# Values made token-major by VectorE's 32x32 block transposition and DMAs by way of DRAM, in a decoder layer on one core

## The chip, the core and the metric

The kernel runs on one core of a Trainium2 chip. A core has five engines with instruction streams of their own: TensorE (PE in the profile: matrix products from SBUF into PSUM; PEld is its weight load), VectorE (DVE), ScalarE (ACT), GpSimd (POOL) and SyncE (SP, which here only issues DMAs). Each engine works its instructions off in order and waits on semaphores for the others. PSUM has eight banks of 128 partitions x 512 numbers. The metric is the device time of one execution in microseconds (us). The kernel before takes 1237.49 us (median of 3 runs, 1237.15 to 1237.61).

## The reference, cut to what matters

One decoder layer on 272 tokens (16 learned ones and 256 of the input), width 2048, all in float32. Two groups of heads share one input projection: four mLSTM heads (values 256 wide) and eight retention heads (values 128 wide).

```python
u = rmsnorm(h, norm_mix)
proj = u @ w_in
q_r, k_r, v_r, g_r, q_m, k_m, v_m, o_m, i_pre, f_pre = split(proj)
# retention: rotary(q), rotary(k); P = (q k^T) * decay;  o = P v
ret = head_norm(o, ret_norm) * silu(g_r)
# mLSTM: causal conv of 4 and silu on q, k; P = (q k^T) * exp(D - m)
hm = head_norm((P v) / max(|sum P|, exp(-m)), mlstm_norm) * sigmoid(o_m)
h = h + concat(ret, hm) @ w_out
u = rmsnorm(h, norm_ffn)
gate, val = split(causal_dwconv(u @ w_up, 3 taps))
h = h + (silu(gate) * val) @ w_down
return rmsnorm(h, norm_final)[:, 16:]
```

`head_norm` takes a head's mean over its value columns away and divides by the root of the variance. The kernel computes attention over all 272 tokens at once, without the chunks and the recurrent state.

## The kernel before, in words

**Layout.** Activations lie with features on the 128 partitions and tokens along the free dimension ("feature-major"). A product `project` makes 128 features of 256 to 272 tokens: the 2048 x 128 weight tile comes as two halves of 512 KB. Each half (`load_w`) is loaded into `wraw`, ScalarE rounds it to `whi` (L129), VectorE takes the remainder `wlo` (L131), and TensorE does 24 products of 128x128 weights: 16 with `whi` on the two parts of the activations (L138, L139), 8 with `wlo` (L141). There are 4 buffers of `wraw`, 5 of `whi` and 5 of `wlo`, so loads and rounding can run some halves ahead of TensorE.

**Stages.** First the input is loaded and split, while the products for the gates and for the first mLSTM head's k and q are made (L208 to L235). Then come the projections of the four mLSTM heads and of the eight retention heads. A head's attention (`ml_attend`, `ret_attend`) is written one head later, so that its small steps can run beside the next head's projections. Then the output projection (L536), the up projection with its convolution (L628) and the down projection (L673).

**The factor rstd.** The input's normalisation is applied after the products: `rstd1` (128 copies of the 272 factors) multiplies what is read from PSUM. It comes from the sum of squares: ScalarE squares `hT` (L246), VectorE adds (L249, L254), a product with `inv_dm` (L256) sums over the partitions, and ScalarE and VectorE make the inverse root (L164 to L169, L258). Until `rstd1` is there, no finished projection can leave PSUM. The pool `mm` has four banks: one holds the first head's q, the next three hold its two value tiles and its first gate; the fifth projection, the second gate, needs the bank of q back, which L416 frees.

**Values.** The weighting product `weigh` needs the values with tokens on the partitions ("token-major"). `values` gets them by six products with the identity per mLSTM head and three per retention head (L324, 272 tokens are blocks of 128, 128 and 16) into banks of the pool `at`. VectorE sums each token's values out of PSUM (L327, L328), scales that to minus the mean (L329, L330), and ScalarE copies the values with the mean taken off into the one buffer `vpad` (L333).

**Order.** The program is written head by head, but each engine's order is fixed when it is built, by a list scheduler that plays the program through on durations of its own; `issue_after` and `high_priority` are hints for it. So a change in one place can move instructions of others. Buffers (`bufs`) are reused in turn, each by a wait for the last reader.

Of the kernel before, what the change touches and what calls it, by code (L numbers as in the profile page):

```python
# [16 lines left out]
P = 128  # L17
# [6 lines left out]
NQ = T - T0  # L24
# [59 lines left out]
def trunk(ctx: ExitStack, tc: tile.TileContext, io, out: bass.AP):  # L84
    nc = tc.nc

    def pool(name, bufs, **kw):
        return tc.tile_pool(name=name, bufs=bufs, **kw)
# [4 lines left out]
    at = ctx.enter_context(pool("at", 4, space=PSUM))  # L93

# [112 lines left out]
    with pool("sq", 1, side="right") as sqp:  # L207
        for k0, k1 in [(0, 1), (1, 2)] + [(k, k + 2) for k in range(2, KT, 2)]:  # L208
            n = k1 - k0
            nc.sync.dma_start(hT[:, k0:k1, :], io["xT"][:, k0:k1, :])  # L210
            if k0 == 0:
                nc.sync.dma_start(par[:, 0:KT], io["par"][:, 0:KT])
            raw = wpool.tile([P, 2, W0], F32, name="wraw", bufs=4)[:, :n, :]
            last_load = nc.sync.dma_start(raw, io["w0"][:, k0:k1, :])
            for k in range(k0, k1):
                nc.scalar.activation(xh[:, k, :], hT[:, k, :], AF.Copy, scale=pcol("gmix", k))
                nc.vector.scalar_tensor_tensor(out=xl[:, k, :], in0=hT[:, k, :], scalar=pcol("gmix", k),
                                               in1=xh[:, k, :].bitcast(F32), op0=ALU.mult, op1=ALU.subtract)

            hi = wpool.tile([P, 2, W0 + GW], F32R, name="whi", bufs=5)[:, :n, :]  # L220
            copied = nc.scalar.copy(hi[:, :, 0:W0], raw)
            lo = wpool.tile([P, 2, 2 * P], F32R, name="wlo", bufs=5)[:, :n, :]
            nc.vector.tensor_tensor(out=lo, in0=raw[:, :, 0 : 2 * P], in1=hi[:, :, 0 : 2 * P].bitcast(F32), op=ALU.subtract)
            parted = nc.vector.tensor_tensor(out=hi[:, :, W0:], in0=raw[:, :, 2 * P :], in1=hi[:, :, 2 * P : W0].bitcast(F32), op=ALU.subtract)
            for k in range(k0, k1):
                i = k - k0
                first, last = k == 0, k == KT - 1
                for j, (ps, t0) in enumerate(((k_ps, 0), (q_ps, TQ))):
                    w = hi[:, :, j * P : (j + 1) * P], lo[:, :, j * P : (j + 1) * P]
                    mmk(ps[:, : T - t0], w, [(i, k)], lambda k: xh[:, k, t0:], lambda k: xl[:, k, t0:], 0, KT - 1)  # L230
                if not last:
                    nc.tensor.matmul(gates_ps[:, :T], hi[:, i, 2 * P :], xh[:, k, :], start=first, stop=False)
                nc.tensor.matmul(gates_ps[0:GW, :T], hi[:, i, 2 * P : W0], xl[:, k, :], start=False, stop=False)
                if last:
                    nc.tensor.matmul(gates_ps[:, :T], hi[:, i, 2 * P :], xh[:, k, :], start=False, stop=True)  # L235
        with tc.issue_after(last_load.ins):
            nc.sync.dma_start(par[:, KT:NPAR0], io["par"][:, KT:NPAR0])

        v0_ps = project(next(tiles), xh, xl, 0)
# [12 lines left out]
        with tc.high_priority():  # L252
            for n in (2, 1):
                nc.vector.tensor_tensor(out=sum4[:, 0:n, :], in0=sum4[:, 0:n, :], in1=sum4[:, n : 2 * n, :], op=ALU.add)  # L254
            ms = at.tile([P, 512], F32, name="atps")
            nc.tensor.matmul(ms[:, :T], inv_dm, sum4[:, 0, :], start=True, stop=True)  # L256
            r = rsqrt_m2(wk, ms[:, :T], T, squared)
            nc.vector.tensor_scalar(out=rstd1, in0=r[:, :T], scalar1=-0.5, scalar2=None, op0=ALU.mult)  # L258
# [12 lines left out]
    rB, rA, rM, rm, rones = map(row, ("rB", "rA", "rM", "rm", "rones"))  # L271
# [41 lines left out]
    def values(vts):  # L313

        w = P * len(vts)
        blocks = ((0, P), (P, P), (2 * P, CC))
        pss = [at.tile([P, 512], F32, name="atps"), None]
        if 3 * w > 512:
            pss[1] = at.tile([P, 512], F32, name="atps")
        where = []  # L320
        for b, (s0, n) in enumerate(blocks):
            ps, c0 = (pss[1], 0) if (b == 2 and pss[1] is not None) else (pss[0], b * w)
            for j, vt in enumerate(vts):
                nc.tensor.transpose(ps[0:n, c0 + j * P : c0 + (j + 1) * P], vt[:, s0 : s0 + n], ident)  # L324
            where.append(ps[0:n, c0 : c0 + w])
        nm = wk.tile([P, 3], F32, name="nm")
        nc.vector.reduce_sum(nm[:, 0:2], pss[0][:, 0 : 2 * w].rearrange("p (a e) -> p a e", a=2), axis=mybir.AxisListType.X)  # L327
        nc.vector.reduce_sum(nm[0:CC, 2:3], where[2], axis=mybir.AxisListType.X)  # L328
# [3 lines left out]
        for b, (s0, n) in enumerate(blocks):  # L332
            nc.scalar.activation(v[0:n, b, :], where[b], AF.Identity, bias=nm[0:n, b : b + 1])  # L333
        return v
# [44 lines left out]
    def ret_project(h):  # L379
        decay = wk.tile([P, ABC], F32, name="e")  # L380
        nc.gpsimd.dma_start(decay, io["decay"][h])
# [12 lines left out]
    def ret_attend(h, kT, qT, vT, g, decay):  # L394
        v = values([vT])
# [43 lines left out]
    def ml_attend(h, kT, qT, vTs, gs):  # L439
        v = values(vTs)  # L440
# [32 lines left out]
        for j in range(2):  # L473
            o = weigh(lambda b: v[:, b, j * P : (j + 1) * P], pT)
            hj = wk.tile([P, NQ], F32, name=f"hj{j}", bufs=1)
# [315 lines left out]
```

## Time and profile before

One profiled execution, and three timed ones.

| What | Value |
|---|---|
| timed, median of 3 (range) | 1237.49 us (1237.15 to 1237.61) |
| the profiled execution, its time | 1237.72 us |
| its span, from first to last instruction | 1236.0 us |
| PE busy, share of the span | 1225.0 us, 99% |
| DVE, ACT, POOL busy | 832.6, 656.9, 66.8 us |
| mean granted TensorE clock | 0.998 |
| DMA, mean over the span | 181 GB/s |
| products with the identity for the values (L324) | 48, of 273 ns each, overlapping |

A row of the timeline has the start, the length (both us), the engine, the line, the operation, output<-input, shapes, and xN for N merged instructions; in square brackets the idle time before it and what ended it. Products overlap: each is some 0.28 us long, but the next one starts 0.12 us after it. A row of the windows has the window (us from the span's start), its length, and then busy time and instruction count of each engine, the granted clock, the DMA share and GB/s.

### The profile page before, as it was taken

What the parts mean: (1) busy time and instruction counts of PE and PEld (TensorE: products, weight loads), DVE (VectorE), ACT (ScalarE), POOL (GpSimd) and SP (SyncE); (2) the same over time, 40 slices, a digit from 0 to 9 for tenths busy, and PEclk for the clock granted to TensorE, in tenths of its full rate; (3) what the DMA queues carried; (4) which work ended last, traced back from release to release, by engine and by line L of the source; (5) the groups of instructions that cost most, each with busy time, mean ns of one, the idle gap of its engine ahead of it and who ended that gap; (6) DMA issues with size and microseconds to landing.
All of it is one profiled execution on the core that took longest, in us unless ns stands there. A gap on an engine that the chain in (4) does not pass through costs nothing.

```text
span 1236.0 us, 22256 instructions
## 1 busy us (share of the span) xinstructions
PE 1225.0 (99%) x9086; PEld 1174.6 (95%) x9086; DVE 832.6 (67%) x1227; ACT 656.9 (53%) x880; POOL 66.8 (5%) x71
## 2 busy tenths in 40 slices
PE   9999999999999999999999999999999999999997
PEld 9999999999999999999999998888999999998886
DVE  7957777766665766778878764445677677674452
ACT  8756756555556556555555543334555555554442
POOL 0200011111110110000000000000000000000000
PEclk9999999999999999999999999999999999999999
DMA  8755555555554656555556556566565555566661
GB/s 271 256 185 154 161 154 161 172 174 161 177 167 132 207 186 212 184 185 179 184 183 185 180 183 187 187 187 188 187 186 176 185 187 177 183 187 182 187 210 69
DMA packets 63687, 224.30 MB, mean 181 GB/s; under 512 B 7392, under 2 KB 8544, under 8 KB 63456
## 3 DMA queue, kind: packets, MB, share of 16 engines
q1 hardware_dynamic: 62640, 219.59, 57.0%
q0 software_dynamic: 656, 2.76, 0.8%
q8 instruction: 71, 1.16, 0.4%
q10 hardware_dynamic: 288, 0.52, 0.1%
q14 instruction: 32, 0.26, 0.1%
HBM read 220.75 MB, written 2.10 MB: 180 GB/s over the span
## 4 chain that ended last, share of the span: by engine, by line
PE 97%; DVE 1%; DMA 1%; ACT 1%; issue 0%; SPq 0%; DVEq 0%; ACTq 0%
PE mmps L138 24%; PE mmps L139 24%; PE mmps L141 24%; PE atps L658 7%; PE atps L659 7%; PE atps L662 7%; PE atps L347 1%; PE atps L339 0%; DMA wraw<-in_w 0%; PE atps L324 0%; DMA wraw<-in_wi 0%; PE atps L348 0%; DVE wlo L131 0%; PE atps L340 0%; ACT whi L129 0%
## 5 line engine op out<-in xcount | busy, mean ns | idle before, releaser
L129 ACT CAST whi<-wraw 128x1024 fp32r<-128x1024 f32 x404 | 423.2, 1049 | 475.5 <-PE mmps L139 255.4
L131 DVE TENSOR_TENSOR wlo<-wraw,whi 128x1024 fp32r<-128x1024 f32 x404 | 495.0, 1226 | 192.4 <-ACT whi L129 187.3
L139 PE MATMUL mmps<-ul,whi 128*128 128x258 f32 x1408 | 345.8, 283 | 0.0
L138 PE MATMUL mmps<-uh,whi 128*128 128x258 f32 x1408 | 345.5, 282 | 0.0
L138 PEld LDWEIGHTS mmps<-uh,whi 128*128 128x128 f32 x1408 | 266.1, 189 | 0.1
L139 PEld LDWEIGHTS mmps<-ul,whi 128*128 128x128 f32 x1408 | 265.1, 188 | 0.1
L138 PE MATMUL mmps<-xh,whi 128*128 128x272 f32 (+2 forms) x880 | 223.5, 287 | 0.4 <-DVE cx L416 0.4
L139 PE MATMUL mmps<-xl,whi 128*128 128x272 f32 (+2 forms) x880 | 223.2, 287 | 0.0
L141 PE MATMUL mmps<-uh,wlo 128*128 128x258 f32 x1408 | 198.9, 284 | 0.0
L141 PEld LDWEIGHTS mmps<-uh,wlo 128*128 128x128 f32 x1408 | 182.4, 189 | 0.0
L138 PEld LDWEIGHTS mmps<-xh,whi 128*128 128x128 f32 x880 | 165.6, 188 | 0.6 <-issue 0.6
L139 PEld LDWEIGHTS mmps<-xl,whi 128*128 128x128 f32 x880 | 166.0, 189 | 0.0
L658 PE MATMUL atps<-whi,mh 128*128 128x512 f32 (+1 forms) x360 | 140.5, 391 | 0.0
L659 PE MATMUL atps<-whi,ml 128*128 128x512 f32 (+1 forms) x360 | 140.2, 390 | 0.0
L141 PE MATMUL mmps<-xh,wlo 128*128 128x272 f32 (+2 forms) x880 | 129.1, 285 | 0.0
L141 PEld LDWEIGHTS mmps<-xh,wlo 128*128 128x128 f32 x880 | 116.4, 188 | 0.1
L662 PE MATMUL atps<-wlo,mh 128*128 128x512 f32 (+1 forms) x360 | 110.8, 388 | 0.0
L572 DVE TENSOR_TENSOR cu<-mmps,rstd 128x258 f32<-128x258 f32 x88 | 37.6, 427 | 97.5 <-PE mmps L141 97.0
L658 PEld LDWEIGHTS atps<-whi,mh 128*128 128x128 f32 x360 | 67.6, 188 | 15.7
L662 PEld LDWEIGHTS atps<-wlo,mh 128*128 128x128 f32 x360 | 67.1, 188 | 16.1
L659 PEld LDWEIGHTS atps<-whi,ml 128*128 128x128 f32 x360 | 67.6, 188 | 15.1
L139 PE MATMUL mmps<-mixl,whi 128*128 128x258 f32 x256 | 63.1, 283 | 0.0
(210 smaller groups left out, 1038.5 us busy)
## 6 DMA issues: line engine op xcount, KB each, us to landing
wraw<-in_wu SPq DMA_DIRECT2D x176, 512.0 KB, 3.5
wraw<-in_wi SPq DMA_DIRECT2D x108, 512.0 KB, 3.6
wraw<-in_wd SPq DMA_DIRECT2D x88, 512.0 KB, 3.5
wraw<-in_wo SPq DMA_DIRECT2D x32, 512.0 KB, 3.6
wraw<-in_w SPq DMA_DIRECT2D x7, 320.0 KB, 5.2
hT<-in_xT SPq DMA_DIRECT2D x7, 272.0 KB, 5.7
e<-in_decay POOLq DMA_DIRECT2D x8, 209.0 KB, 3.4
gfin<-in_gfin POOLq DMA_DIRECT2D x1, 1024.0 KB, 5.8
```

Source lines behind the costliest of these rows:

```text
L129: nc.scalar.copy(hi, raw)
L131: nc.vector.tensor_tensor(out=lo, in0=raw, in1=hi.bitcast(F32), op=ALU.subtract)
L138: nc.tensor.matmul(ps, hi[:, k, :], xh(kk), start=kk == first, stop=False)
L139: nc.tensor.matmul(ps, hi[:, k, :], xl(kk), start=False, stop=False)
L141: nc.tensor.matmul(ps, lo[:, k, :], xh(kk), start=False, stop=kk == last)
L347: nc.tensor.matmul(ps[:, 0:NQ], lhs(0), pT[:, 0:CA], start=True, stop=False)
L572: nc.vector.tensor_tensor(out=u, in0=ps[:, :NQ], in1=rstd2, op=ALU.mult)
L658: nc.tensor.matmul(ps, mh[:, k, rows], hi[:, i, cols], start=k == 2 * first, stop=False)
L659: nc.tensor.matmul(ps, ml[:, k, rows], hi[:, i, cols], start=False, stop=False)
L662: nc.tensor.matmul(ps, mh[:, k, rows], lo[:, i, cols], start=False, stop=k == 2 * last + 1)
```

## The change

`values` no longer uses TensorE. A new function `turned` is called where the values' projection has been scaled: VectorE's `transpose` turns every 32x32 block of the feature-major values (128 x 256, and 128 x 32 for the last 32 tokens) into `vb`. One DMA on GpSimd's queue writes `vb` to a DRAM buffer `away`. Four DMAs on the same queue read from it, one for each group of 32 partitions, which puts the blocks in their places, and a fifth reads the 16 last tokens. They land in `v4`, which `values` then reads from SBUF in place of PSUM: the sums, the scaling and the copies into `vpad` are as before, with other strides and two or three axes per instruction.

To make room in SBUF, the sum of squares at the start is made in another way: eight squares of two tiles each and seven sums of 128x544 into a buffer of `v4` (and one last of 128x272), where there were four squares of four tiles, three sums of 128x1088 and one each of 544 and 272. `rones`, `rm` and `hj` share buffers. All lines after the first change move: L129, L131, L138, L139 and L141 of before are L130, L132, L139, L140 and L142 now.

```diff
+    dram = ctx.enter_context(pool("dram", 2, space=bass.MemoryType.DRAM))
...
-        sum4 = None
-        for k in range(0, KT, 4):
-            sq = rope if k % 8 else sqp.tile([P, 4, T], F32, name="sq" if k else "sum4")
-            with tc.issue_after(copied.ins):
-                squared = nc.scalar.activation(sq, hT[:, k : k + 4, :], AF.Square)
-            if k:
-                with tc.issue_after(parted.ins), tc.high_priority():
-                    nc.vector.tensor_tensor(out=sum4, in0=sum4, in1=sq, op=ALU.add)
-            else:
-                sum4 = sq
-        with tc.high_priority():
-            for n in (2, 1):
-                nc.vector.tensor_tensor(out=sum4[:, 0:n, :], in0=sum4[:, 0:n, :], in1=sum4[:, n : 2 * n, :], op=ALU.add)
...
+    sum2 = wk.tile([P, 768], F32, name="v4")[:, : 2 * T].rearrange("p (a t) -> p a t", a=2)
+    for k in range(0, KT, 2):
+
+        sq = rope[:, k % 4 : k % 4 + 2, :] if k else sum2
+        with tc.issue_after(copied.ins):
+            squared = nc.scalar.activation(sq, hT[:, k : k + 2, :], AF.Square)
+        if k:
+            with tc.issue_after(parted.ins), tc.high_priority():
+                nc.vector.tensor_tensor(out=sum2, in0=sum2, in1=sq, op=ALU.add)
+    with tc.high_priority():
+        nc.vector.tensor_tensor(out=sum2[:, 0, :], in0=sum2[:, 0, :], in1=sum2[:, 1, :], op=ALU.add)
...
-    def values(vts):
-
-        w = P * len(vts)
-        blocks = ((0, P), (P, P), (2 * P, CC))
-        pss = [at.tile([P, 512], F32, name="atps"), None]
...
-                nc.tensor.transpose(ps[0:n, c0 + j * P : c0 + (j + 1) * P], vt[:, s0 : s0 + n], ident)
...
+    def turned(vts):
+
+        n = len(vts)
+
+        vb = wk.tile([P, 2 * 288], F32, name="vb", bufs=1)[:, : 288 * n]
+        for j, vt in enumerate(vts):
+            o = vb[:, : 256 * n].rearrange("p (a j b f) -> p j b a f", a=4, j=n, b=2)[:, j]
+            nc.vector.transpose(o, vt[:, 0:256].rearrange("p (b a f) -> p b a f", b=2, a=4))
+            nc.vector.transpose(vb[:, 256 * n + 32 * j : 256 * n + 32 * (j + 1)], vt[:, T - 32 : T])
+
+        m = 64 * n
+        away = dram.tile([P, 2 * 288], F32, name="away")[:, : 288 * n]
+        nc.gpsimd.dma_start(away, vb)
+        v4 = wk.tile([P, 768], F32, name="v4")[:, : 384 * n]
+        main, tail = v4[:, : 4 * m].rearrange("r (i x) -> r i x", i=4), v4[0:CC, 4 * m :].rearrange("r (i x) -> r i x", i=4)
+        for a in range(4):
+            nc.gpsimd.dma_start(main[32 * a : 32 * (a + 1)], away[:, a * m : (a + 1) * m].rearrange("(i r) x -> r i x", i=4))
+        nc.gpsimd.dma_start(tail, away[:, 4 * m :].rearrange("(i r) x -> r i x", i=4)[32 - CC :])
+        return v4, n
+
+    def values(v4, n):
...
+        nc.vector.reduce_sum(nm[:, 0:2], v4[:, : 2 * w].rearrange("p (x b f) -> p b x f", b=2, f=32), axis=mybir.AxisListType.XY)
+        nc.vector.reduce_sum(nm[0:CC, 2:3], tail, axis=mybir.AxisListType.X)
...
+        to = v.rearrange("p b (j i f) -> p b i j f", j=n, i=4)
+        for b in range(2):
+            nc.scalar.activation(to[:, b], main[:, b], AF.Identity, bias=nm[:, b : b + 1])
...
-        vT = scaled(project(next(tiles), xh, xl, 0), 0, "vT0")
+        vT = turned([scaled(project(next(tiles), xh, xl, 0), 0, "vT0")])
...
+        vTs = turned(vTs)
```

The change also moves instructions that it does not touch. The first place is TensorE around the product with `inv_dm`, the first step from the sum of squares to `rstd1`. Before, it stands inside the fourth half's products with `wlo` (`wlo_545`):

```order
L141 MATMUL mmps_510<-xh_94,wlo_545 128x272 x4
L256 MATMUL atps_434<-sum4_423,inv_dm_75 128x272
L141 MATMUL mmps_510<-xh_94,wlo_545 128x272 x4
L139 MATMUL mmps_573<-xl_95,whi_576 128x258
L138 MATMUL mmps_573<-xh_94,whi_576 128x258
```

With the change, behind the fifth half's `wlo` (`wlo_595`) and five products of the sixth half:

```order
L142 MATMUL mmps_590<-xh_96,wlo_595 128x258 x8
L139 MATMUL mmps_590<-xh_96,whi_623 128x258
L140 MATMUL mmps_590<-xl_97,whi_623 128x258
L253 MATMUL atps_439<-v4_422,inv_dm_77 128x272
L140 MATMUL mmps_590<-xl_97,whi_623 128x258
```

Counted from the first product of the first value tile, 101 products stood ahead of it; now 125 do.

The second place is VectorE, from the last sum to the instruction that frees the bank of q (`cx<-mmps`, L416 before, L428 now; `rstd` is `rstd1`, `g` and `qT` of 4x272 are the rows of the two mLSTM gates). Before:

```order
L254 TENSOR_TENSOR sum_423<-sum_423 128x272
L131 TENSOR_TENSOR wlo<-wraw,whi 128x1024 x3
L168 SCALAR_TENSOR_TENSOR rt<-atps,rt 128x272
L169 SCALAR_TENSOR_TENSOR r_436<-rt,r_436 128x272
L258 TENSOR_SCALAR rstd_83<-r_436 128x272
L278 TENSOR_TENSOR g_455<-g_455,rstd_83 4x272
L278 TENSOR_TENSOR qT<-qT,rstd_83 4x272
L420 TENSOR_TENSOR cx<-atps,rstd_83 128x272
L416 TENSOR_TENSOR cx<-mmps,rstd_83 128x262
```

Now:

```order
L251 TENSOR_TENSOR v_422<-v_422 128x272
L132 TENSOR_TENSOR wlo<-wraw,whi 128x1024 x3
L169 SCALAR_TENSOR_TENSOR rt<-atps,rt 128x272
L170 SCALAR_TENSOR_TENSOR r_441<-rt,r_441 128x272
L255 TENSOR_SCALAR rstd_85<-r_441 128x272
L132 TENSOR_TENSOR wlo<-wraw,whi 128x1024
L276 TENSOR_TENSOR g_459<-g_459,rstd_85 4x272
L276 TENSOR_TENSOR qT<-qT,rstd_85 4x272
L432 TENSOR_TENSOR cx<-atps,rstd_85 128x272
L428 TENSOR_TENSOR cx<-mmps,rstd_85 128x262
```

One remainder of a weight half (L132) now stands between `rstd1` and the first instruction that uses it.

The third place is VectorE and GpSimd in a retention head in the middle. On VectorE the values have been scaled and, one remainder of weights later, turned (the last row of that stands first here); the sums of the landed values (L337) stand behind the next head's gate (`g0`), the weighting of the head before (`ppad`) and three remainders, and ahead of the remainder `vl` of the variance (L369), which TensorE uses:

```order
L319 STREAM_TRANSPOSE vb_3032<-vT0_3030 128x32
L132 TENSOR_TENSOR wlo_3250<-wraw_3246,whi_3248 128x1024
L308 TENSOR_TENSOR g0_3104<-mmps_3043,rstd1_85 128x258
L132 TENSOR_TENSOR wlo_3287<-wraw_3283,whi_3285 128x1024
L410 TENSOR_TENSOR ppad_105<-atps_3115,e_2521 128x402
L411 TENSOR_TENSOR ppad_105<-atps_3115,e_2521 16x16
L132 TENSOR_TENSOR wlo_3317<-wraw_3313,whi_3315 128x1024
L337 TENSOR_REDUCE nm_3420<-v4_3037 128x2
L338 TENSOR_REDUCE nm_3420<-v4_3037 16x1
L339 TENSOR_SCALAR nm_3420<-nm_3420 128x2
L340 TENSOR_SCALAR nm_3420<-nm_3420 16x1
L369 TENSOR_TENSOR vl_3128<-s2_3125,vh_3127 128x258
```

On GpSimd the six DMAs stand between the head's rotary sum and the load of the next decay matrix, all in one queue with the next head's sums; the first of the four reads (L327) waits until the write (L323) has landed:

```order
L388 TENSOR_TENSOR qT_2963<-qT_2963,cx_2964 128x258
L323 DMA away_3035<-vb_3032 128x288
L327 DMA v4_3037<-away_3035 32x4x64 x4
L328 DMA v4_3037<-away_3035 16x4x32
L393 DMA e_3147<-in_decay 128x418
L388 TENSOR_TENSOR kpad1_103<-kpad1_103,cx_3210 128x272
L388 TENSOR_TENSOR qT_3276<-qT_3276,cx_3277 128x258
```

Before, the queue had only the decay's load and the two sums. The values' way thus begins as soon as they have been scaled: two projections ahead of the head's scores in an mLSTM head, one in a retention head. The products with the identity stood right ahead of the scores.

More of the change, by code (lines that the diff above doesn't have):

```diff
@@ new lines, in trunk @@
+    for k0, k1 in [(0, 1), (1, 2)] + [(k, k + 2) for k in range(2, KT, 2)]:
+        n = k1 - k0
+        nc.sync.dma_start(hT[:, k0:k1, :], io["xT"][:, k0:k1, :])
+        if k0 == 0:
+            nc.sync.dma_start(par[:, 0:KT], io["par"][:, 0:KT])
+        raw = wpool.tile([P, 2, W0], F32, name="wraw", bufs=4)[:, :n, :]
+        last_load = nc.sync.dma_start(raw, io["w0"][:, k0:k1, :])
+        for k in range(k0, k1):
+            nc.scalar.activation(xh[:, k, :], hT[:, k, :], AF.Copy, scale=pcol("gmix", k))
+            nc.vector.scalar_tensor_tensor(out=xl[:, k, :], in0=hT[:, k, :], scalar=pcol("gmix", k),
+                                           in1=xh[:, k, :].bitcast(F32), op0=ALU.mult, op1=ALU.subtract)
+        hi = wpool.tile([P, 2, W0 + GW], F32R, name="whi", bufs=5)[:, :n, :]
+        copied = nc.scalar.copy(hi[:, :, 0:W0], raw)
+        lo = wpool.tile([P, 2, 2 * P], F32R, name="wlo", bufs=5)[:, :n, :]
+        nc.vector.tensor_tensor(out=lo, in0=raw[:, :, 0 : 2 * P], in1=hi[:, :, 0 : 2 * P].bitcast(F32), op=ALU.subtract)
+        parted = nc.vector.tensor_tensor(out=hi[:, :, W0:], in0=raw[:, :, 2 * P :], in1=hi[:, :, 2 * P : W0].bitcast(F32), op=ALU.subtract)
+        for k in range(k0, k1):
+            i = k - k0
+            first, last = k == 0, k == KT - 1
+            for j, (ps, t0) in enumerate(((k_ps, 0), (q_ps, TQ))):
+                w = hi[:, :, j * P : (j + 1) * P], lo[:, :, j * P : (j + 1) * P]
+                mmk(ps[:, : T - t0], w, [(i, k)], lambda k: xh[:, k, t0:], lambda k: xl[:, k, t0:], 0, KT - 1)
+            if not last:
+                nc.tensor.matmul(gates_ps[:, :T], hi[:, i, 2 * P :], xh[:, k, :], start=first, stop=False)
+            nc.tensor.matmul(gates_ps[0:GW, :T], hi[:, i, 2 * P : W0], xl[:, k, :], start=False, stop=False)
+            if last:
+                nc.tensor.matmul(gates_ps[:, :T], hi[:, i, 2 * P :], xh[:, k, :], start=False, stop=True)
@@ new lines, in trunk @@
+    with tc.issue_after(last_load.ins):
+        nc.sync.dma_start(par[:, KT:NPAR0], io["par"][:, KT:NPAR0])
+    v0_ps = project(next(tiles), xh, xl, 0)
+    sum2 = wk.tile([P, 768], F32, name="v4")[:, : 2 * T].rearrange("p (a t) -> p a t", a=2)
[6 more added lines that the diff above has]
+                nc.vector.tensor_tensor(out=sum2, in0=sum2, in1=sq, op=ALU.add)
@@ L259, in trunk @@
+    with tc.high_priority():
+        nc.vector.tensor_tensor(out=sum2[:, 0, :], in0=sum2[:, 0, :], in1=sum2[:, 1, :], op=ALU.add)
+        ms = at.tile([P, 512], F32, name="atps")
+        nc.tensor.matmul(ms[:, :T], inv_dm, sum2[:, 0, :], start=True, stop=True)
+        r = rsqrt_m2(wk, ms[:, :T], T, squared)
+        nc.vector.tensor_scalar(out=rstd1, in0=r[:, :T], scalar1=-0.5, scalar2=None, op0=ALU.mult)
     with tc.issue_after(last_load.ins):
@@ L270, in trunk @@
     row = lambda name: pa.tile([MH, T], F32, name=name)
-    rB, rA, rM, rm, rones = map(row, ("rB", "rA", "rM", "rm", "rones"))
+    rB, rA, rM = map(row, ("rB", "rA", "rM"))
+    rones, rm = (wk.tile([P, T], F32, name=f"hj{i}", bufs=1)[0:MH, :] for i in range(2))
     ri, rf, ra, re = (wk.tile([P, T], F32, name=i)[0:MH, :] for i in ("g0", "qT", "vT0", "vT1"))
```

56 lines of the change are left out of this document (7 added, 49 removed).

## The prediction

> **What bounds the kernel now.** I read the page's busy shares first, then TensorE's own waits, then the windows.
>
> ```profile
> span 1236.0 us, 22256 instructions
> PE 1225.0 (99%) x9086; PEld 1174.6 (95%) x9086; DVE 832.6 (67%) x1227; ACT 656.9 (53%) x880; POOL 66.8 (5%) x71
> ...
> L129 ACT CAST whi<-wraw 128x1024 fp32r<-128x1024 f32 x404 | 423.2, 1049 | 475.5 <-PE mmps L139 255.4
> ...
> PE mmps L138 <- DVE cx L416: 0.4, 1, 0.4
> PE atps L339 <- ACT floor L456: 0.2, 1, 0.2
> ...
> 42.20:60.00 17.80, 17.80 (x145) 17.62 (x146) 17.63 (x27) 15.95 (x23) 6.73 (x4) 1.00 0.67 209
> 272.00:298.00 26.00, 26.00 (x212) 25.87 (x211) 17.06 (x28) 14.42 (x21) 4.01 (x3) 1.00 0.57 172
> ```
>
> TensorE sets the end. Once the first weights are in, it waits twice, 0.4 and 0.2 us. A product taken off TensorE therefore comes off the time, and a gap made in it is added. ScalarE's rounding of weights waits mostly for TensorE to free a buffer (255.4 us), so the weights are some halves ahead. In a retention head (272 to 298) VectorE and the DMAs have room; between 42 and 60 VectorE is full.
>
> **What is removed: 48 products with the identity.**
>
> ```profile
> 84.25 0.82 PE L324 MATMUL atps<-ident,vT 128*128 128x128 f32 x6
> 84.83 0.36 PE L443 MATMUL atps<-parts,sel 128*128 128x258 f32 x1
> 85.03 0.28 PE L454 MATMUL atps<-parts,sel 128*128 128x258 f32 x1
> ...
> 220.03 0.49 PE L324 MATMUL atps<-ident,vT 128*128 128x128 f32 x3
> 220.36 0.60 PE L339 MATMUL atps<-qT,kpad 128*128 128x258 f32 x2
> ```
>
> From the first to the instruction behind them, six take 0.58 us and three 0.33. L443 behind them takes 0.20 until the next starts, where ordinary products take 0.12, so up to 0.08 more goes in an mLSTM head. Four times 0.58 to 0.66 and eight times 0.33 is 5.0 to 5.3 us. I take **5.2**. No wait of TensorE stood there, so nothing else hides it.
>
> **What moves at the start.** This is the change's other half. These are before's steps from the sum of squares to the bank that TensorE waits for.
>
> ```profile
> 23.32 0.29 PE L138 MATMUL mmps<-xh,whi 128*128 128x272 f32 x1
> 35.94 0.62 PE L256 MATMUL atps<-sum,inv_dm 128*128 128x272 f32 x2
> 40.73 1.00 PE L141 MATMUL mmps<-xh,wlo 128*128 128x258 f32 x7
> 42.12 0.36 PE L138 MATMUL mmps<-xh,whi 128*128 128x258 f32 x1 [0.38 <-DVE cx L416]
> ...
> 36.23 1.05 ACT L129 CAST whi<-wraw 128x1024 fp32r<-128x1024 f32 x1 [0.24 <-DMA wraw<-in_wi]
> 37.19 0.48 ACT L164 ACTIVATE r<-atps,epsc 128x272 f32<-128x272 f32 x1
> ...
> 38.63 0.44 DVE L168 SCALAR_TENSOR_TENSOR rt<-atps,rt 128x272 f32<-128x272 f32 x1
> 39.92 0.43 DVE L278 TENSOR_TENSOR g<-g,rstd 4x272 f32<-4x272 f32 x1
> 40.28 1.01 DVE L278 TENSOR_TENSOR qT<-qT,rstd 4x272 f32<-4x272 f32 x1
> 41.56 0.41 DVE L416 TENSOR_TENSOR cx<-mmps,rstd 128x262 f32<-128x262 f32 x1
> 41.90 1.20 DVE L131 TENSOR_TENSOR wlo<-wraw,whi 128x1024 fp32r<-128x1024 f32 x1
> 43.64 1.68 DVE L131 TENSOR_TENSOR wlo<-wraw,whi 128x1024 fp32r<-128x1024 f32 x1
> ```
>
> TensorE made 101 products from 23.32 to 35.94, 0.125 each. Now 125 stand ahead of the product with `inv_dm`: it starts at 23.32 + 15.6 = 38.95 and is done 0.62 later, at 39.57. The sums do not hold it: eight squares and eight adds end well before 38, as VectorE has only six remainders of 1.2 us between them. Before, ScalarE was busy with a rounding until 37.28 and began L164 only at 37.19; now it is free by about 39.5 and begins at 39.6. Its three steps take 1.44 (37.19 to 38.63) and VectorE's three 1.29 (38.63 to 39.92): `rstd1` can be used at 42.35. Now comes the moved remainder, 1.20, to 43.55, then two gate rows and the k tile, 1.64 (39.92 to 41.56), to 45.2, and L428 with TensorE's start behind it, 0.56 (41.56 to 42.12). The fifth projection starts at **45.75 instead of 42.12: 3.6 us lost**, since everything ahead of it on TensorE is the same work and ends at 41.7 as before.
>
> Bounds: the second gate row took 1.01 where the first took 0.43; if it doesn't, the loss is 3.0. Above, the remainder may take 1.68, and its half must have been loaded and rounded by 42.35:
>
> ```profile
> 41.12 1.05 ACT L129 CAST whi<-wraw 128x1024 fp32r<-128x1024 f32 x1 [0.25 <-DMA wraw<-in_wi]
> 43.08 1.04 ACT L129 CAST whi<-wraw 128x1024 fp32r<-128x1024 f32 x1
> ```
>
> Before, the tenth half was rounded at 41.12, as soon as it had landed, and the eleventh, the one that counts now, at 43.08. The sums are shorter now and free buffers for loads a little sooner, so I have it landed by 41. If it comes as late as before, the loss is 5.4. So 3.0 to 5.4; the steps above are nearest to 3.6.
>
> Behind the gap a second, smaller wait follows.
>
> ```profile
> 47.47 1.28 ACT L282 ACT_TABLE_LOAD   x1
> 53.22 0.70 DVE L284 TENSOR_TENSOR_SCAN rB<-rones,qT 4x272 f32<-4x272 f32 x1
> 54.97 0.48 DVE L285 SCALAR_TENSOR_TENSOR rA<-g,par,rB 4x272 f32<-4x272 f32 x1
> ...
> L568 DVE STREAM_TRANSPOSE hn<-hT 32x512 f32<-32x512 f32 x32 | 20.7, 681 | 0.2
> L327 DVE TENSOR_REDUCE nm<-atps 128x2 f32<-128x256 f32 x8 | 3.3, 417 | 0.0
> ```
>
> The three products of `rA` with `ident` now stand 65 products behind the resume, at about 53.6. ScalarE needs, from 45.25, two copies, two table loads of 1.28 and four steps of some 0.4: 50.5. VectorE then has a step, a value tile's turn, a step, the scan of 0.70, a remainder and `rA`: 3.8, so 54.3. I take **0.8**, between 0 and 1.5 (GpSimd multiplies the rotary table then, and VectorE's 1.68 above fell into that).
>
> **What is added.** VectorE: 16 value tiles, each turned in two instructions. The trace has L568, 512 numbers per partition in 0.68; for 256 I take 0.42 as for a sum of 256, and 0.15 for the 32. In heads that is under 1.2 of VectorE's idle 9 us; between 42 and 60, where there is none, it is in the 0.8. DMA: at most 295 KB written and as much read per head, against a share of 0.57 with 512 KB every 3 us: hidden. GpSimd: six issues a head.
>
> ```profile
> L381 POOL DMA_DIRECT2D e<-in_decay x8: 553/554/722, 130.8 to 352.9; - x8
> DMA to landing us min/median/max: 2.8/3.4/4.3
> ...
> out<-hn SPq DMA_DIRECT2D x2, 128.0 KB, 1.9
> ...
> 252.67 0.29 PE L349 MATMUL atps<-ppad,vpad 128*128 128x16 f32 x2
> 259.45 0.28 PE L360 MATMUL atps<-vl,inv_ret 128*128 128x258 f32 x1
> 266.39 0.44 DVE L310 TENSOR_TENSOR vT<-mmps,rstd 128x272 f32<-128x272 f32 x1 [0.58 <-PE mmps L141]
> 272.12 0.43 DVE L310 TENSOR_TENSOR g<-mmps,rstd 128x258 f32<-128x258 f32 x1 [1.52 <-PE mmps L141]
> ```
>
> In a retention head, from the end of the values' projection: scaling, a remainder and the turn, 2.2; the write and its landing, 3.4; four issues, the last 1.65 after the first; 3.4 to land: 10.7 (7.7 with hops of 1.9, 12.5 with 4.3). The gate's projection covers 5.7 of it (266.39 to 272.12). What queues behind the sum on VectorE is `vl`, whose product on TensorE stands 115 products after the values' projection, at 14.2; the sums and `vl` need 2.0 of that, so landing up to 12.2 costs nothing. The remainders that wait too are halves ahead. On GpSimd the six issues end 7.8 after the projection, the next sum that is needed comes after 11. An mLSTM head has two projections, 11.5, for the same way. Added: **0**.
>
> [...] The decay's issue took 0.55 to 0.72 with VectorE two thirds busy. [...]
>
> **Sum.** -5.2 + 3.6 + 0.8 = -0.8, from the profiled execution's 1237.7 (0.2 above the median of 1237.5): **1236.9**. Its own range is 1237.7 - 5.3 + 3.0 = 1235.4 to 1237.7 - 5.0 + 5.4 + 1.5 = 1239.6.
>
> **Rivals.** *The clock falls in the gap.*
>
> ```profile
> 1.06 4.60 PE L200 MATMUL atps<-ones 128*128 128x128 f32 x20 [1.06 <-DVE ones L107]
> 5.34 0.45 PE L138 MATMUL atps<-xh,whi 128*128 128x272 f32 x1
> ...
> 1227.43 0.40 PE L662 MATMUL atps<-wlo,mh 128*128 128x256 f32 x2
> ...
> 1230.50:1231.00 0.50, 0.00 (x0) 0.00 (x0) 0.50 (x3) 0.22 (x1) 0.00 (x0) 0.86 0.00 0
> 1231.00:1231.50 0.50, 0.00 (x0) 0.00 (x0) 0.47 (x2) 0.00 (x0) 0.00 (x0) 0.50 0.67 217
> ```
>
> At the end the granted clock fell to half 3.0 us after the last product (1227.83 to 1230.86). The gap is 41.74 to 45.75, 4.0 us. At the kernel's start 20 products of 128 columns took 4.3 us, 0.21 each where L324's take 0.11, so half speed may last that long; 4.3 us at half speed lose 2.1, of which 0.8 covers the wait for `rA`: 1238.3. One fall doesn't tell when in a gap it comes. [...]
>
> *The gap at the start does not grow*, because `rstd1` is not what holds TensorE at 42.12. Then 1237.7 - 5.2 = 1232.5. Against it: the wait names L416.
>
> *The values land late* (the other side): from 12.2 us on, `vl` and so TensorE wait in each retention head. Two hops of 4.3 and the tail's 0.55 give 13.1: 0.9 late, eight times, 7.2: 1244. For it, six small transfers in a row; against it, a median of 3.4 for 209 KB.
>
> *TensorE gains nothing where products go*, since it then waits there for scores or weights instead: 1237.7 + 4.4 = 1242.1. Against it: it waited 0.2 us in all heads.
>
> **Chances.** Forecast 0.50, clock 0.20, no gap 0.10, late values 0.12, nothing gained 0.08. A difference under 0.2%, 2.5 us, cannot be told from none here. Faster (below 1235.0): no gap and 0.03 of the forecast, 0.13. Slower (above 1240.0): late values, nothing gained, 0.05 of the clock's and the forecast's high ends: 0.25. Same: 0.62. The range 1234.6 to 1242.0 leaves out the no-gap and the late case.
>
> **What would show it.** TensorE's waits should name the bank of q (L428) with 3.4 to 4.4 us near 42 to 46, then `rA` with under 1.5 us; L253 at 39; no L324. `vpad`'s copies should come before the weighting in every head, with L337 waiting on a DMA at most 2 us; products at 0.12 right behind the gap tell the clock apart. I am wrong if that gap is under 2 us, or if waits of TensorE appear in the heads.

## The result, and the profile after

The changed kernel is slower: **1253.3 us** (median of 5 runs, 1250.33 to 1255.23) against 1237.6 (5 runs, 1237.15 to 1237.87), a ratio of 1.0125 with a 95% interval of 1.0114 to 1.0136. Forecast were 1236.9 us and no change. The profiled execution is the fastest of the five, 1250.33 us with a span of 1248.5; it is 12.6 us longer than the profiled one before. Of the runs below, one execution of experiment 4 ran at a mean granted clock of 0.752 and took 1471.27 us; it is left out of that experiment's figures.

First come the page's busy times and TensorE's waits in the changed kernel, with VectorE's wait for the values as the last row (a row of waits has the us in total, the number of waits and the longest).

```profile
span 1248.5 us, 22360 instructions
PE 1226.1 (98%) x9038; PEld 1174.7 (94%) x9038; DVE 839.0 (67%) x1262; ACT 663.2 (53%) x887; POOL 99.5 (8%) x143
...
PE mmps L139 <- DVE cx L428: 5.1, 1, 5.1
PE atps L480 <- DVE ppad L473: 4.8, 2, 3.0
...
PE atps L372 <- DVE vl L369: 1.1, 1, 1.1
...
PE atps L359 <- ACT vpad L344: 0.7, 1, 0.7
...
DVE nm L337 <- DMA v<-away: 26.3, 9, 7.0
```

48 products are gone (9086 to 9038), and yet TensorE is busy for 1.1 us more than before. So some products must have become longer. Once the first weights are in, it waits 11.7 us where it had waited 0.6: 5.1 at the start, as forecast in kind, and 6.6 in the heads, where the forecast had none. VectorE stood 26.3 us at one instruction, the sum of the landed values (L337), in nine heads.

The windows show which products became longer: those behind each of the three longest waits. The column behind POOL's is the granted clock.

```profile
42.00:46.00 4.00, 0.00 (x0) 0.00 (x0) 3.91 (x6) 1.03 (x1) 2.82 (x3) 1.00 0.74 261
46.40:46.60 0.20, 0.00 (x0) 0.00 (x0) 0.20 (x2) 0.10 (x1) 0.20 (x1) 0.66 0.74 164
47.00:49.50 2.50, 2.50 (x12) 2.50 (x13) 2.50 (x8) 2.47 (x5) 0.45 (x1) 0.50 0.28 115
49.80:50.00 0.20, 0.20 (x3) 0.20 (x2) 0.20 (x2) 0.20 (x1) 0.00 (x0) 0.81 0.00 0
...
138.60:138.80 0.20, 0.20 (x2) 0.18 (x1) 0.20 (x1) 0.00 (x0) 0.20 (x1) 0.56 0.00 0
139.00:142.00 3.00, 2.97 (x12) 2.64 (x11) 1.35 (x4) 0.26 (x1) 0.86 (x2) 0.50 0.79 296
143.00:146.00 3.00, 3.00 (x27) 3.00 (x26) 3.00 (x6) 1.54 (x3) 0.00 (x0) 1.00 0.02 3
182.80:183.00 0.20, 0.20 (x2) 0.17 (x2) 0.20 (x1) 0.00 (x0) 0.20 (x1) 0.99 0.00 0
...
183.20:186.20 3.00, 2.85 (x11) 2.56 (x10) 1.35 (x4) 0.22 (x1) 0.91 (x2) 0.50 0.83 285
```

The clock fell to 0.5 at 46.46, 138.62 and 183.00 and was back at 49.88, 142.04 and 186.41, each time 3.41 us later (worked out from the share of short windows at full clock, as of the three of 0.2 us around a fall and the one at 49.80). A product of 258 columns then starts every 0.21 us (12 in 2.5 us above), not every 0.12.

Where the time went can be read by setting the traces side by side: the projections' products (L138, L139 and L141 before; L139, L140 and L142 now) come in the same number, 7680, and the same order. This is the start of the same product in a later kernel less its start before, in us. The last row is the kernel of experiment 4 below, which mends both places.

```
time before          40    45    58    85    95   125   135   165   174   243   295   348   end
changed kernel      0.1   6.1   6.3   6.5   5.7   6.0   9.0   9.3  13.5  12.0  12.9  12.5  12.6
both mended         0.0   0.0  -0.8   0.3  -0.5  -0.2  -1.1  -0.8  -1.6  -3.2  -3.8  -4.3  -5.3
```

The changed kernel loses 6.1 us at the start, 3 and 4 us at two steps (125 to 135, 165 to 174), which are the attention of two mLSTM heads, and little else: 0.9 at a retention head (243 to 295). Between these it gains, slowly, what the removed products took.

**The start.** This is the chain from ScalarE's first step towards `rstd1` (L165) to the fifth projection, in the timelines of ScalarE, VectorE and TensorE.

```profile
39.39 1.06 ACT L130 CAST whi<-wraw 128x1024 fp32r<-128x1024 f32 x1 [0.24 <-DMA wraw<-in_wi]
40.35 0.47 ACT L165 ACTIVATE r<-atps,epsc 128x272 f32<-128x272 f32 x1
...
41.78 0.44 DVE L169 SCALAR_TENSOR_TENSOR rt<-atps,rt 128x272 f32<-128x272 f32 x1
...
43.06 1.23 DVE L132 TENSOR_TENSOR wlo<-wraw,whi 128x1024 fp32r<-128x1024 f32 x1
44.21 0.99 DVE L276 TENSOR_TENSOR g<-g,rstd 4x272 f32<-4x272 f32 x1
45.13 0.98 DVE L276 TENSOR_TENSOR qT<-qT,rstd 4x272 f32<-4x272 f32 x1
46.04 0.42 DVE L432 TENSOR_TENSOR cx<-atps,rstd 128x272 f32<-128x272 f32 x1
46.39 0.41 DVE L428 TENSOR_TENSOR cx<-mmps,rstd 128x262 f32<-128x262 f32 x1
...
46.95 0.55 PE L139 MATMUL mmps<-xh,whi 128*128 128x258 f32 x1 [5.07 <-DVE cx L428]
```

The chain is the one that the prediction laid out, 1.2 us later at its end: ScalarE was in a rounding until 40.35, and the two gate rows (L276) took 0.9 us each.

**The heads.** This is one of the two stretches, in the timelines of VectorE, then GpSimd, then TensorE. The values of the third mLSTM head are made while the second head's attention is worked on. `away<-vb` is the write to DRAM, `v<-away` are the reads.

```profile
121.54 0.43 DVE L308 TENSOR_TENSOR vT<-mmps,rstd 128x272 f32<-128x272 f32 x1
...
127.14 1.23 DVE L132 TENSOR_TENSOR wlo<-wraw,whi 128x1024 fp32r<-128x1024 f32 x1 [0.34 <-ACT whi L130]
134.19 0.69 DVE L337 TENSOR_REDUCE nm<-v 128x2 f32<-128x512 f32 x1 [5.83 <-DMA v<-away]
134.79 0.42 DVE L308 TENSOR_TENSOR g<-mmps,rstd 128x258 f32<-128x258 f32 x1
135.12 0.48 DVE L458 SCALAR_TENSOR_TENSOR e<-atps,acol,big 128x258 f32<-128x258 f32 x1
...
137.47 0.55 DVE L473 SCALAR_TENSOR_TENSOR ppad<-atps,e 128x402 f32<-128x402 f32 x1
...
124.18 0.58 POOL L323 DMA_DIRECT2D away<-vb  x1 [17.96 <-DVE vb L319]
129.29 2.18 POOL L327 DMA_DIRECT2D v<-away  x4 [4.53 <-DMA away<-vb]
...
130.63 0.29 PE L353 MATMUL atps<-qT,kpad 128*128 128x16 f32 x2
138.08 0.48 PE L480 MATMUL atps<-ppad,ones 128*128 128x114 f32 x2 [1.79 <-DVE ppad L473]
```

The values were scaled at 121.54 and could be summed at 134.19, 12.65 later. VectorE reached that sum at 128.36 and stood for 5.83 us. Behind it in VectorE's queue were the gate, three steps of `e`, a remainder and `ppad` of the second head, whose scores TensorE had finished at about 130.9 (L353); TensorE needs that `ppad` next (L480). The landed values, for which all of this waited, are the third head's, and TensorE has no use for them until that head's own weighting, a head later.

### The profile page after: what moved, and what is told of

Same layout as the page of the kernel before. It is cut to its first block, busy times and chain, and to the rows that moved or that the text cites. A ratio compares the mean times of both kernels' runs of the same rounds, so it can differ in the third digit from the quotient of the medians.

```text
span 1248.5 us, 22360 instructions
## 1 busy us (share of the span) xinstructions
PE 1226.1 (98%) x9038; PEld 1174.7 (94%) x9038; DVE 839.0 (67%) x1262; ACT 663.2 (53%) x887; POOL 99.5 (8%) x143
## 4 chain that ended last, share of the span: by engine, by line
PE 81%; ACT 1%; DVE 1%; DMA 1%; issue 1%; POOL 0%; DVEq 0%; ACTq 0%; POOLq 0%
PE mmps L142 20%; PE mmps L139 20%; PE mmps L140 20%; PE atps L671 7%; PE atps L672 7%; PE atps L675 7%; PE atps L359 0%; DMA away<-vb 0%; DMA v<-away 0%; DVE wlo L132 0%; ACT whi L130 0%; PE atps L351 0%; PE atps L360 0%; ACT L166 0%; ACT L165 0%
## 5 line engine op out<-in xcount | busy, mean ns | idle before, releaser
L130 ACT CAST whi<-wraw 128x1024 fp32r<-128x1024 f32 x404 | 423.0, 1049 | 458.4 <-PE mmps L140 238.9
L132 DVE TENSOR_TENSOR wlo<-wraw,whi 128x1024 fp32r<-128x1024 f32 x404 | 496.7, 1231 | 185.5 <-ACT whi L130 181.0
L140 PE MATMUL mmps<-ul,whi 128*128 128x258 f32 x1408 | 345.8, 283 | 0.0
L139 PE MATMUL mmps<-uh,whi 128*128 128x258 f32 x1408 | 345.5, 282 | 0.0
L139 PEld LDWEIGHTS mmps<-uh,whi 128*128 128x128 f32 x1408 | 266.1, 189 | 0.1
L140 PEld LDWEIGHTS mmps<-ul,whi 128*128 128x128 f32 x1408 | 265.1, 188 | 0.1
L139 PE MATMUL mmps<-xh,whi 128*128 128x272 f32 (+2 forms) x880 | 225.3, 288 | 5.1 <-DVE cx L428 5.1
L140 PE MATMUL mmps<-xl,whi 128*128 128x272 f32 (+2 forms) x880 | 224.1, 288 | 0.0
L142 PE MATMUL mmps<-uh,wlo 128*128 128x258 f32 x1408 | 198.9, 284 | 0.0
L142 PEld LDWEIGHTS mmps<-uh,wlo 128*128 128x128 f32 x1408 | 182.4, 189 | 0.0
L139 PEld LDWEIGHTS mmps<-xh,whi 128*128 128x128 f32 x880 | 166.7, 189 | 5.3 <-issue 5.3
L140 PEld LDWEIGHTS mmps<-xl,whi 128*128 128x128 f32 x880 | 166.6, 189 | 0.0
L142 PE MATMUL mmps<-xh,wlo 128*128 128x272 f32 (+2 forms) x880 | 130.2, 286 | 0.0
L142 PEld LDWEIGHTS mmps<-xh,wlo 128*128 128x128 f32 x880 | 117.0, 188 | 0.0
L603 POOL TENSOR_TENSOR hn<-hn,gfin 128x512 f32<-128x512 f32 (+1 forms) x7 | 9.7, 1395 | 742.1 <-ACT junk L599 742.1
```

The costliest lines, as they stand in the source:

```text
L130: nc.scalar.copy(hi, raw)
L132: nc.vector.tensor_tensor(out=lo, in0=raw, in1=hi.bitcast(F32), op=ALU.subtract)
L139: nc.tensor.matmul(ps, hi[:, k, :], xh(kk), start=kk == first, stop=False)
L140: nc.tensor.matmul(ps, hi[:, k, :], xl(kk), start=False, stop=False)
L142: nc.tensor.matmul(ps, lo[:, k, :], xh(kk), start=False, stop=kk == last)
L603: nc.gpsimd.tensor_tensor(out=h, in0=h, in1=gfin[:, c0:c1], op=ALU.mult)
```

## Experiments

**1. The start alone.** The kernel before, with only the new sum of squares (in the pool of the old one). The values stay products with the identity.

```diff
-        sum4 = None                      # four squares of 128x1088, three sums of 128x1088, one of 544, one of 272
+        sum2 = sqp.tile([P, 768], F32, name="v4")[:, : 2 * T].rearrange("p (a t) -> p a t", a=2)
...
```

> The kernel before, with the new sum of squares (eight squares of two tiles, seven sums of 128x544) as its only edit; the values stay products with the identity. Theory A: the start's loss comes from this edit alone, by the order it gives (the product with inv_dm 24 products later, one remainder ahead of the gate rows), and the gap of 5 us is followed by one window of 3.41 us at half clock. Then TensorE waits 4.5 to 5.2 us for the bank of q, the next 12 products run at 0.21, and the time is 1237.6 + 4.7 + 1.4 = 1243.7, between 1242.5 and 1245. Rival B: the gap comes from what the values add on VectorE and GpSimd around 45 to 60. Then the time stays within 1 us of 1237.6.

Measured: 1244.58 us (1243.23 to 1244.73) against 1237.77; ratio 1.0049 [1.0036, 1.0061]. TensorE's longest wait and the windows around its end and behind it:

```profile
PE mmps L138 <- DVE cx L413: 5.0, 1, 5.0
...
45.20:45.40 0.20, 0.00 (x0) 0.00 (x0) 0.20 (x1) 0.00 (x0) 0.20 (x2) 0.73 0.22 41
45.40:51.80 6.40, 5.32 (x25) 5.35 (x26) 4.85 (x14) 5.67 (x9) 1.70 (x3) 0.50 0.22 76
52.00:52.20 0.20, 0.20 (x3) 0.20 (x3) 0.20 (x2) 0.20 (x1) 0.00 (x0) 0.71 0.00 0
53.00:56.00 3.00, 3.00 (x27) 3.00 (x25) 2.93 (x6) 2.95 (x6) 0.00 (x0) 1.00 0.26 60
```

This is as theory A has it. The start's loss needs nothing of the values; it comes from the edit that made room for them. Here the low clock lasted 6.8 us, from 45.29 to 52.12 by the shares of the two 0.2 us windows, and the product offset behind it is 6.9 us rather than 6.3.

**2. The old sum back.** The changed kernel, with the old sum of squares in a pool on the left side, in the space where `mixh` and `mixl` come later.

```diff
+    with pool("sq", 1, side="left") as sqp:
...
+        sum4 = None
...
+    mixp_cm = pool("mixp", 1, side="left")
```

> The changed kernel, with the old sum of squares (four squares of four tiles) back, in space that is free until the heads begin; the values still go by VectorE and DRAM. Theory A: the gap at 42 to 47 and the half-clock window behind it go, and nothing in the heads changes: 1253.3 - 6.1 = 1247, between 1244 and 1250. Rival B (the values make the gap): stays at 1251 or above.

Measured: 1246.76 us (1245.28 to 1247.85); ratio to before 1.0071 [1.0057, 1.0084]. The wait for the bank of q is 0.5 us, against 0.4 before the change; the waits for `ppad` are still there (5.7 us in two, 2.55 and 3.11). This is as theory A has it: the start gives 6.5 us back (1253.3 to 1246.76), and the heads lose what they lost.

**3. The sums behind the weighting.** The changed kernel; `values` is called behind the instruction that writes `ppad`, and its sums are kept behind it on VectorE. The new start stays.

```diff
-        v = values(*vTs)
...
+        last = nc.vector.scalar_tensor_tensor(out=pT[0:CC, AB:], in0=sps[0:CC, AB:ABC], scalar=sc, in1=e[0:CC, AB:], ...)
+        v = values(*vTs, last)
...
+        with tc.issue_after(after.ins):
             nc.vector.reduce_sum(nm[:, 0:2], ...)
```

> The changed kernel, with the sums of the landed values ordered behind the weighting (ppad) on VectorE in each head; nothing else is changed. Theory A: in the mLSTM heads the landed values are not what TensorE needs first; the wait of the sums for the DMA holds up the scores' instructions queued behind it on VectorE. Then TensorE's waits for ppad (1.8 and 3.0 us) and the half-clock windows behind them (1.7 us each) go: 1253.3 less 8 to 11, so 1242 to 1245.5. Rival C: the values themselves are late, or their transfers slow VectorE and the weights down. Then the wait only moves from L480 to the product with vpad, and the time stays above 1249.

Measured: **1238.36 us** (1237.7 to 1242.77, 11 runs); ratio 1.0009 [1.0000, 1.0017]. TensorE's longest waits, and the same stretch on VectorE and TensorE:

```profile
PE mmps L139 <- DVE cx L429: 4.7, 1, 4.7
PE atps L201 <- DVE ones L108: 1.1, 1, 1.1
...
129.65 0.43 DVE L308 TENSOR_TENSOR g<-mmps,rstd 128x258 f32<-128x258 f32 x1 [1.56 <-PE mmps L142]
129.99 0.48 DVE L458 SCALAR_TENSOR_TENSOR e<-atps,acol,big 128x258 f32<-128x258 f32 x1
...
132.31 0.58 DVE L473 SCALAR_TENSOR_TENSOR ppad<-atps,e 128x402 f32<-128x402 f32 x1 [0.30 <-issue]
132.80 0.15 DVE L474 SCALAR_TENSOR_TENSOR ppad<-atps,e 16x16 f32<-16x16 f32 x1
132.88 0.66 DVE L338 TENSOR_REDUCE nm<-v 128x2 f32<-128x512 f32 x1
...
135.10 0.37 PE L481 MATMUL atps<-ppad,ones 128*128 128x114 f32 x2
```

No wait of TensorE is left in any head, and VectorE no longer waits for a DMA of the values. The sums at 132.88 are those of the head whose `ppad` stands ahead of them; its values landed a head ago. So it is the place of the sums in VectorE's queue that lets a way of this length hold TensorE up. The expected range, 1242 to 1245.5, was worked out from the profiled execution and was missed: the gain by medians is 14.9 us, not 8 to 11. The other executions of the changed kernel had lost more than the profiled one: their times, 1252.99 to 1255.23, go with mean clocks of 0.989 to 0.991, against 0.994. One fall of 3.41 us takes 3.41 x 0.5 / 1250 = 0.0014 from the mean clock, so by this estimate they had some two to four such falls more. Where these were, no trace shows.

**4. Both mended.** Experiments 2 and 3 in one kernel.

> The changed kernel with both edits: the old sum of squares, and the sums of the values behind the weighting. Theory A: both losses go and the removed products remain as a gain: 1237.6 - 5.2 = 1232.4, up to 1234.5 if the two short waits in the retention heads (1.1 and 0.7 us) stay. By rivals B and C it would be above 1245.

Measured: **1232.48 us** (1232.28 to 1232.98, four runs); ratio 0.9956 [0.9942, 0.9969]. This beats both kernels. TensorE's waits, all of them:

```profile
PE atps L196 <- DVE ones L108: 1.1, 1, 1.1
PE atps L139 <- ACT whi L217: 1.0, 2, 0.5
PE mmps L139 <- DVE cx L433: 0.4, 1, 0.4
```

The gain is of the size of the removed products: the offset of the last product is -5.3 us in the table above, where 5.2 had been worked out for them.

**5. The gap filled.** Experiment 1, with 18 products of `ones` put into the gap (each of them is two rows of the trace).

```diff
+            if h == j == 0:
+                with tc.issue_after(last_mm.ins), tc.high_priority():
+                    for _ in range(18):
+                        nc.tensor.matmul(ms[:, T : T + P], ones, ones, start=True, stop=True)
```

> The kernel before with the new sum of squares alone, as in the first experiment (1244.6), and 18 more products of ones into a free part of a bank, 3.9 us of TensorE's work, in the gap of 5 us ahead of the fifth projection; their result is not used. Theory A: the products behind the gap run at half speed because TensorE stood idle in it. With the gap filled the clock stays at 1.0, the fifth projection starts no earlier, and the time is 1237.7 + 4.7 = 1242.4, between 1241.7 and 1243.2. Rival D: the clock falls for another reason at this place (the start-up, or VectorE and ScalarE busy at once), or is not what the last 2 us are. Then it stays at 1244.6, or above.

Measured: 1241.68 us (1241.4 to 1242.59); ratio to before 1.0033 [1.0020, 1.0045]; 2.9 us less than experiment 1, by medians of the two. TensorE and the windows:

```profile
41.83 4.18 PE L438 MATMUL atps<-ones 128*128 128x128 f32 x36
46.28 0.36 PE L138 MATMUL mmps<-xh,whi 128*128 128x258 f32 x1 [0.26 <-DVE cx L414]
...
46.50:50.00 3.50, 3.50 (x31) 3.50 (x31) 3.18 (x8) 3.42 (x6) 0.40 (x2) 1.00 0.16 61
```

The fifth projection starts as late as without them (46.28; 46.48 in experiment 1), but at full clock: 31 products in 3.5 us. So here TensorE's idleness is what lowers the clock (0.50 from 46 to 50 in experiment 1, 1.00 from 46.5 to 50 here), and the start's loss in experiment 1 is 4.0 us of waiting (1241.68 - 1237.69) and 2.9 of slow products.

**6. The mLSTM heads alone.** As 4, with the sums behind `ppad` in the four mLSTM heads only.

```diff
-        v = values(*vT, last)      # ret_attend
+        v = values(*vT)            # ret_attend, ahead of the scores
```

> The changed kernel with the old sum of squares, and the sums of the values behind the weighting in the four mLSTM heads alone; in the retention heads the order is left to the scheduler, as in the changed kernel. Theory A: the loss of the heads is that of the mLSTM heads, where the sums stand ahead of the scores. Then at most the two short waits of the retention heads come back: 1232.5 to 1235. Rival E: the retention heads, of which one or two waited 1.1 us in the profiled execution, carry a good part of the loss in the others (by half-clock windows). Then 1236 to 1242.

Measured: 1233.75 us (1232.9 to 1234.32); ratio 0.9966 [0.9954, 0.9978]. The retention heads cost 1.3 us; the profiled execution shows one wait of 0.7 there, for `vpad`. The mLSTM heads are 13.0 of the 14.3 us between experiments 2 and 4.

**7 and 8. A longer way.** The values take one more hop, from one DRAM buffer to another, in all heads but the last; once in the version that mends both, and once with the old sum of squares alone.

```diff
         nc.gpsimd.dma_start(away, vb)
+        if hop:
+            away, first = dram.tile([P, 2 * 288], F32, name="away2")[:, : 288 * n], away
+            nc.gpsimd.dma_start(away, first)
```

> The version with the old sum of squares and the sums behind the weighting in each head (1232.5), with one more hop for the values: from one DRAM buffer to another, about 4 us, in all heads but the last. Theory A: a head's values are not needed before the next head's end, so 4 us more cost nothing: 1232.5, up to 1234. Rival C (it is the length of the way, or the transfers, that costs): some us more per head, 1245 or above.

Measured: 1232.36 us (1232.19 to 1233.48); ratio 0.9959 [0.9946, 0.9971]. This is the version with both places mended. From the write's issue to the first read, 6.5 to 10.1 us pass in the eleven heads with the hop, where it was 3.3 to 4.9 without; no time is lost.

> The changed kernel with the old sum of squares (1246.8) and the same additional hop. The scheduler counts the hop and so puts the sums behind the scores' instructions by itself. Theory A, that the sums' place in VectorE's queue is what costs: although the values come 4 us later, the time falls, to between 1232.5 and 1240. Rival C, that the values' lateness costs: 4 us more in each of ten heads or so, above 1255.

Measured, with the old sum of squares alone: 1239.75 us (1237.25 to 1241.94, 11 runs); ratio 1.0014 [1.0005, 1.0023]. A way that is some 4 us longer makes the kernel **7 us faster** than experiment 2. VectorE and TensorE while the second head's attention is worked on, and a window around the longest wait:

```profile
127.38 0.58 DVE L480 SCALAR_TENSOR_TENSOR ppad<-atps,e 128x402 f32<-128x402 f32 x1 [0.31 <-issue]
127.88 0.15 DVE L481 SCALAR_TENSOR_TENSOR ppad<-atps,e 16x16 f32<-16x16 f32 x1
133.02 0.69 DVE L344 TENSOR_REDUCE nm<-v 128x2 f32<-128x512 f32 x1 [4.99 <-DMA v<-away]
...
132.67 0.51 PE L488 MATMUL atps<-late,ones 128*128 128x144 f32 x2 [1.29 <-POOL late L485]
...
172.80:176.20 3.40, 1.86 (x15) 1.86 (x16) 1.97 (x5) 0.81 (x2) 1.39 (x4) 1.00 0.35 90
```

With the hop counted, the scheduler put the sums behind `ppad` by itself, in all four mLSTM heads. VectorE still waits 5 us for the values, but with less behind it that TensorE needs soon. What is left is GpSimd's queue: `late`, which TensorE needs, now stands behind the reads there, and its three waits are 3.8 us. The clock is 1.00 in the window around the longest wait, and its mean over the profiled execution is 0.998, as before the change. Rival C, that lateness itself costs, would have made this the slowest of all.

## Why the prediction was wrong

**The step that failed** is the last sentence on what is added: "An mLSTM head has two projections, 11.5, for the same way. Added: **0**." Two things in it were wrong, the length of the way and the deadline that it was held against.

The way took 12.2 to 13.9 us in the four mLSTM heads, from the scaling to the sums, and about 0.4 more from the end of the projection, where the term said 10.7. In the third head, whose rows are above, it was 3.0 us from that end to the write (2.2 forecast), 5.1 from the write's issue to the first read (3.4), 1.6 from the first to the fourth read's issue (1.65) and 3.3 to the last landing (3.4): 13.0 in all.

The deadline was taken from the wrong place. For the retention heads the prediction had looked up what queues behind the sum on VectorE, and found `vl`, needed at 14.2. For the mLSTM heads it did not, and took the time until the head's own scores. There the sums stand ahead of `e` and `ppad` of the head before, and TensorE waited for that `ppad` 1.79 us in one head and 2.99 in the next. If the sums had begun as much earlier, it would not have waited; that puts the real limit at an estimated 11.2 us from the end of the projection, in both. (In the second head a way of 12.2 held nothing up; `ppad` had time to spare there.) So 11.5 was close to it by luck, and a way of 10.7 would just have fitted; a way of 13.0 or 14.2 did not. With the sums behind `ppad` the same way costs nothing (experiments 3 and 4), and a longer one neither (experiment 7).

Behind each of the two waits the clock fell as well, which the forecast's sum had nowhere. By medians the heads cost 14.3 us (experiment 2 less 4) where 0 had been forecast, and the start 6.8 (experiment 1) where 4.4 had been. The rival "the values land late" had the right mechanism, a sum that waits and holds up what queues behind it, but its place was the retention heads, where one wait of 1.1 us and one of 0.7 came; the larger waits came in two mLSTM heads.

The deadline of a value is here not when TensorE wants it. It is when the next instruction behind its first reader is wanted.

**The retention heads** lost little, by a thin margin: a way of 10.9 to 13.1 us (10.7 forecast, 12.2 the limit), one wait for `vl` of 1.1 behind a way of 12.8, and 1.3 us in all by experiment 6. The way was longer than forecast here too, but mostly near the limit.

**The start** was right in its mechanism, and in the two steps that cause it: the product with `inv_dm` at 38.98 (38.95 forecast), and one remainder ahead of the gate rows. The resume came at 46.95 where 45.75 was worked out. 0.7 of it is ScalarE, which the prediction had free at 39.5; a rounding from 39.39 held it until 40.35. 0.55 is the gate rows: 0.9 us each to the next start, where before the first took 0.36 and the second 0.9. GpSimd's multiplication of the rotary table is beside them. These are the rows of before and of the changed kernel:

```profile
39.96 8.87 POOL L499 TENSOR_TENSOR rope<-rope,rstd 128x272 f32<-128x272 f32 x4 [38.57 <-DVE rstd L258]
```

```profile
43.18 4.27 POOL L512 TENSOR_TENSOR rope<-rope,rstd 128x272 f32<-128x272 f32 x4 [41.78 <-DVE rstd L255]
```

Before, the first gate row started 0.04 ahead of GpSimd's (39.92) and was quick (0.36 to the next start); now both start behind it (44.21, 45.13) and are slow (0.9), while the next one, with an operand from PSUM, is quick (0.35). What makes the gate rows slow is not shown: no run here isolates it. The second term, 0.8 us for `rA`, did not come: `rA` was done at 55.3, 1 us later than forecast, but TensorE came to it only at 56.3, behind a later resume and the slow products. By waiting alone the start cost 4.0 us (experiment 5) where 4.4 had been forecast.

**The clock** was a rival and not the forecast. In all three traces that had this gap unfilled the clock was low behind it: at 0.50 from 46.46 to 49.88 in the changed kernel, from 45.29 to 52.12 in experiment 1, and over a window from 47 to 50 in experiment 3. The sum of that rival, 1238.3, is close to what experiment 3 measured, 1238.4: a start with the clock's fall and heads without loss. That the two agree so well is partly luck: the wait there was 4.7 us, 4.3 more than before where 3.6 had been forecast, and the rival had taken 4.3 us of low clock, which lasted 3.41 behind the same gap in the changed kernel. The prediction read the one fall at the end of the trace before as "3.0 us after the last product"; in the heads, falls came with a wait of 1.79 us (at 138.62, 0.5 us after the wait's end) and with one of 2.99 (at 183.00). The wait of 1.14 at 268 had none (1.00 from 267 to 272), and neither had the 1.54 us that TensorE stood idle between 172.80 and 176.20 in experiment 8 (1.00 over that window). The three falls are 92.16 and 44.38 us apart, which is 27.0 and 13.0 times the 3.41 us that each lasted. What sets the moment of a fall, and how much idleness it takes, no run here isolates; nor does one show why the low clock lasted 6.8 us in experiment 1, where it came 1.2 us before the resume, and 3.41 in the changed kernel, where it came 0.5 us before.

**What is removed** was right: 5.2 forecast, 5.3 measured as the offset at the end of the version that mends both. The turn took 0.44 and 0.16 us where 0.42 and 0.15 had been estimated. GpSimd's issues of the values' write and reads took 0.55 to 0.75 us, against 0.55 to 0.72 for the decay's issue before, so none was held up.

## What to carry to other kernels

Where a product is replaced by a way through DRAM, look up for **every** kind of stage what stands behind the first reader of the landed data on its engine, in the order of the program as built; a reader that waits for a DMA should stand behind everything that is needed sooner. A scheduler that places the reader too early makes everything behind it wait, and here a longer transfer, which made it place the reader later, gave the faster program. An edit that only makes room can cost more than the change it serves gains (6.8 us against 5.3 here). And where TensorE is 99% busy, a gap can cost a second time in slow products: here 3.41 us at half clock with gaps of 1.8 and 3.0 us, by estimate up to 1.7 us each (3.41 x 0.5), and 2.9 us by experiment 5 with a gap of 5.0.

## What the runs showed of the hardware that was not expected

- The clock fell to 0.5 for 3.41 us with a gap of 1.8 us (and of 3.0 and 5.1) in the changed kernel, and not with one of 1.1 or 0.7 there or one of 1.5 in experiment 8; a gap of 5.0 us lowered it for 6.8 us in the first experiment. Unused products in that gap kept it at 1.0 (46.5 to 50, experiment 5), and saved 2.9 us.
- Small transfers through DRAM on GpSimd's queue: 3.1 to 5.6 us from the write's issue to the first read, then 2.2 us to issue four reads, and some 2 to 4 us until the sums. In all 10.9 to 13.9 us from the scaling, with a spread of 3 us over twelve heads; in three of them VectorE came to the sums only after the landing.
